# Consecutive dense products to different PSUM banks in a two-layer hybrid network on one core

## The chip, the cores and the metric

The kernel runs on one core of a Trainium2 chip. The metric is the device time of one execution in microseconds (us); the same program was run three times, and one more execution was recorded by the hardware profiler.

## What is computed

Two layers over 256 tokens of 1024 features, in float32. Each layer adds half of a gated feed-forward network, then a mixer, then half of another feed-forward network to `x`:

```python
def swiglu(h, w_gu, w_down):
    g, u = jnp.split(h @ w_gu, 2, axis=-1)
    return (jax.nn.silu(g) * u) @ w_down
...
for l in range(DEPTH):
    x = x + 0.5 * swiglu(rmsnorm(x, ffn1_norm[l]), ffn1_w_gu[l], ffn1_w_down[l])
    ...
    x = x + mix
    x = x + 0.5 * swiglu(rmsnorm(x, ffn2_norm[l]), ffn2_w_gu[l], ffn2_w_down[l])
```

`w_gu` is 1024 x 5632 and `w_down` 2816 x 1024. The even layer's mixer is a gated product along the tokens beside a differential attention; the odd layer's is a latent attention beside a grouped one. Each mixer has one input product from the normed `x` and one output product with a 1024 x 1024 matrix.

## The kernel before

**Accuracy.** TensorE multiplies operands of a float32r type with about 12 bits. So every weight and every activation is split into an upper part (`hi`, or part 0) and the rest (`lo`, or part 1), and a product a·w is summed from three: upper by upper, upper by lower, lower by upper.

**Products.** `dense(b, xh, xl, wh, wl, ...)` issues these three one after the other into one PSUM bank `b`. `wide(b, wh, wl, x2, ...)` does the same with two instructions: the weights' upper part against both parts of the activations side by side (512 columns, filling a bank), then the weights' lower part against the activations' upper part (256 columns, added to the bank's second half). A bank holds 512 float32 a partition; there are eight, named `bank_124` to `bank_131` in the orders below.

**Stages.** A feed-forward network has two. The *gate-up* stage (`ffn`, first loop) takes four tiles of 128 columns at a time, four banks: for each of 8 tiles k of the normed input `xs`, it calls `wide` for each of the four. The *down* stage (second loop) takes one tile t of 128 output features at a time, one bank, and calls `wide` for each of 22 tiles k of the gated values `hs`, which lie in the tile `region`. `evac` and `add` empty the banks on ScalarE and VectorE. `add` writes `x`, and then `after` (`normed`) makes the next stage's `xs` tile and adds to the sum of squares. A mixer's input product (`block`) has one bank for each half of the tokens; for each k it calls `dense` for the first half, then for the second. `out_product` has four banks, two output tiles to a bank, and goes through the rows of the weights in two halves p, all eight tiles t in each. `small` holds two further products of the odd mixer.

**Weights** stream from DRAM by 1 MB loads on SP's queue, in the order in which they are used; ScalarE (`hi`) and VectorE (`lo`) split them by pieces of 1024 elements a partition into two rings of six tiles. A piece has eight chunks of 128 x 128, and `chunk(ids, c)` finds a stream's c-th.

**Order.** All operations are recorded first; `Program.schedule` then starts them by priority and readiness, with a cost for each, and `emit` issues them from one line (L285 before), which is why all rows of the profile have that line. What stands in `prog.together()` stays together on its engine: one call of `dense` or `wide` before. Operations that empty banks, and those of the attentions, have a lead of 20 us over products in their priority.

Of the kernel before, what the change touches and what calls it, by code (L numbers as in the profile page):

```python
# [21 lines left out]
N = 256         # tokens  # L22
# [4 lines left out]
# rsqrt: the first guess's factor, and the constant that yields the guess  # L27
FACTOR, GUESS = 1.5 ** 0.2, 520464320.0

# the order of the mixers' parts: blocks of the input product, heads of the attentions  # L30
EVEN = "k q v u b d10 d00 d11 d01"
ODD = "q k g00 c u0 u1 g01 g11 m00 g10 m10 m01 m11"
SUB, PIECE = 2048, 1024         # elements a partition of a load of weights, and of a piece of it
RAW, RING = 4, 6                # tiles for loads, for pieces
T1, T2 = 6, 9                   # scratch tiles of 256 and of 512 elements
ARENA, ARENA32 = 11264, 5472    # elements a partition for what one part of the network keeps
MOST, SPARE = (6, 8), 2         # banks held by dense products and by others; those kept for the next in turn
# how far operations go before products (ns): those that empty banks, those of attention, the splits of weights
LEAD, LEAD_A, LEAD_W = 20e3, 20e3, 10e3
PATIENCE = 500.0                # for how long VectorE leaves a copy to ScalarE (ns)  # L40
WARM = 8

# columns of gcol: gains that run along the partitions
GC = {"norm": 0, "cq": 48, "bs": 51, "sub": 59, "mq": 60, "mk": 61}
NGC = 64
# columns of grow: gains that run along the free axis, on every partition
GR = {"evq": (0, 64), "evk": (64, 64), "mq": (128, 32), "mk": (160, 32), "gq": (192, 64), "gk": (256, 64), "lam": (320, 256)}
NGR = 576
# columns of rope: cos, -sin, sin of each kind of position
# [3 lines left out]
# ---- operations are recorded, then emitted in the order in which a list scheduler starts them  # L53
class Slot:
    """a view of a tile whose place the scheduler has still to choose among those of its kind"""
# [14 lines left out]
class Kind:  # L70
    """tiles of one size: how many, and how many of them are kept for the next in the recorded order"""
# [10 lines left out]
class Program:  # L82
    """Operations in an order that is right, with what each reads and writes; emitted by priority and readiness."""

    def __init__(self):
        self.ops = []
        self.writer, self.readers = {}, {}
        self.clock = 0.0   # the products' time so far: the base of the priorities
        self.spans = {}
        self.group = None  # L90
        self.slots = {}    # name -> [operations on it, kind, the first of them]
# [70 lines left out]
    def schedule(self):  # L162
        """-> the operations in the order of their starts, and the place of each slot"""
# [12 lines left out]
        wait = {e: [] for e in engs}     # by the time they are ready  # L176
        ready = {e: [] for e in engs}    # by priority
# [16 lines left out]
        def when(o, t):  # L194
            """the time from which the slots that o opens have places, or None"""
# [94 lines left out]
class Engine:  # L290
    """records the calls of one engine's instructions, each with the time that it takes (ns)"""
# [39 lines left out]
class Either:  # L331
    """copies that ScalarE or VectorE can make: the scheduler chooses"""
# [19 lines left out]
def trunk_kernel(ctx: ExitStack, tc: tile.TileContext, a: dict, out: bass.AP):  # L352
# [9 lines left out]
    def lead(ns):  # L362
        """the operations in here go before products recorded up to ns ahead of them"""
# [8 lines left out]
    # ---- memory: fixed tiles, some of them taken in turn  # L372
# [16 lines left out]
    class Arena:  # L389
        """what the parts of the network keep in one region, one part after the other"""  # L390
# [9 lines left out]
    class Taken:  # L400
        """scratch tiles of one kind"""
# [50 lines left out]
    with lead(90e3):  # L452
        # the tensor engine's clock rises with its use: it is kept busy while the first loads are under way
# [4 lines left out]
    # ---- the stream of weights: loaded, then split into two parts of 12 bits each  # L458
    loads, pieces, raws, ready = [], [], [], []

    def load(ap, widths):
        """-> the pieces' numbers"""
# [8 lines left out]
    def first(raw, w, n):  # L471
        """the first two loads of weights, in parts and among those of x"""
# [27 lines left out]
    def weight(i):  # L500
        fetch(i)
        return ready[i]

    # ---- pieces of arithmetic
    def rsqrt(y, s, scale, tile=None):
        """y = (s * scale + EPS) ** -0.5: a guess from the exponent, then a step of third order and one of Newton's.
        The guess is too large by the factor that makes the first step's leading coefficient 1."""
# [13 lines left out]
    def sums(ss, src, scale, n, w):  # L521
        """sums of squares of scale * src over each head's w, src [P, n * w]"""
# [4 lines left out]
    def rsqrt_of(srcs, scales, n, w):  # L527
        """[P, 2, n]: each head's 1 / rms of scale * src, for the two halves"""
# [5 lines left out]
    def split(dst_hi, dst_lo, src, gain=None):  # L534
        """the parts of src, times the gain of each partition"""
# [7 lines left out]
    def dense(b, xh, xl, wh, wl, first, last):  # L543
# [607 lines left out]
```

## Time and profile before

| | us |
|---|---|
| median of three runs | 947.79 (947.45 to 948.05) |
| profiled execution, span from its first to its last instruction | 946.8 |
| two feed-forward stages of it, gate-up and down, from the middle of the run | 122.3 and 62.2 |

The page gives for each engine its busy time and its share of the span; matmuls (PE) and the loads of their stationary operand (PEld) stand apart. A row of the timeline gives the start, the duration and the instruction, written as output<-inputs; a matmul's duration includes its passage through the array, so that neighbours overlap. The page has no time of the profiled execution other than its span.

### The profile page before, as it was taken

How to read it: one execution, taken by the hardware profiler on the slowest of the kernel's cores; microseconds unless marked ns; L12 is line 12 of the kernel's file. 1: busy time of each engine (PE TensorE's matmuls, PEld its weight loads, DVE VectorE, ACT ScalarE, POOL GpSimd, SP SyncE). 2: the span in 40 equal slices, each digit the busy share in tenths (PEclk: the TensorE clock that was granted, in tenths of full speed). 3: DMA queues.
4: the chain of work that ended last, by engine and by line, in shares of the span. 5: the costliest groups of instructions: out<-in, count | busy, mean ns of one | idle time of the engine just before them, and what ended most of it. 6: DMA issues, size and time to landing. Idle time of an engine off the chain costs nothing.

```text
span 946.8 us, 14519 instructions
## 1 busy us (share of the span) xinstructions
PE 938.2 (99%) x5564; PEld 825.4 (87%) x5564; DVE 729.8 (77%) x1332; ACT 546.0 (58%) x932; POOL 29.5 (3%) x57
## 2 busy tenths in 40 slices
PE   8999999999999999999999999999999999999998
PEld 7888888888899888888888888888989988888887
DVE  7997776679989878876688887766888698887651
ACT  7765654446956666654455656544487566565430
POOL 0920000000000000000000000000000000000000
PEclk9999999999999999999999999999999999999999
DMA  8775555553254555555555555554512355555530
GB/s 319 272 262 182 181 197 196 184 178 134 95 214 170 190 188 205 185 178 184 197 179 197 181 202 197 178 183 154 184 59 84 107 185 199 178 192 207 192 107 17
DMA packets 26421, 167.83 MB, mean 177 GB/s; under 512 B 2928, under 2 KB 5104, under 8 KB 7024
## 3 DMA queue, kind: packets, MB, share of 16 engines
q1 hardware_dynamic: 26352, 166.92, 50.1%
q8 instruction: 43, 0.70, 0.3%
q14 instruction: 26, 0.21, 0.1%
HBM read 165.86 MB, written 1.05 MB: 176 GB/s over the span
## 4 chain that ended last, share of the span: by engine, by line
PE 96%; DVE 1%; DMA 1%; ACT 1%; issue 0%; SPq 0%; DVEq 0%; ACTq 0%
PE bank L285 96%; DMA gx<-in_gx 1%; ACT t L285 1%; DVE t L285 0%; DVE sm L285 0%; DVE lo L285 0%; SPq L285 0%; DVE acc L285 0%; DVE region L285 0%; DVE hi L285 0%; ACT L285 0%; ACT hi L285 0%; ACT xs L285 0%; DVE ssg L285 0%; DVE gx L285 0%
## 5 line engine op out<-in xcount | busy, mean ns | idle before, releaser
L285 ACT ACTIVATE hi<-raw 128x1024 fp32r<-128x1024 f32 (+3 forms) x310 | 322.8, 1043 | 316.8 <-PE bank L285 199.0
L285 DVE TENSOR_TENSOR lo<-raw,hi 128x1024 fp32r<-128x1024 f32 (+2 forms) x318 | 382.5, 1204 | 155.9 <-ACT hi L285 150.3
L285 PE MATMUL bank<-xs,hi 128*128 128x512 f32 x1408 | 489.0, 392 | 1.1 <-ACT hi L285 1.1
L285 PE MATMUL bank<-xs,lo 128*128 128x256 f32 x1408 | 394.0, 280 | 1.6 <-DVE lo L285 1.6
L285 PEld LDWEIGHTS bank<-xs,hi 128*128 128x128 f32 x1408 | 264.4, 188 | 59.5 <-ACT hi L285 1.6
L285 PE MATMUL bank<-region,hi 128*128 128x512 f32 (+1 forms) x982 | 296.6, 364 | 0.0
L285 PEld LDWEIGHTS bank<-xs,lo 128*128 128x128 f32 x1408 | 264.3, 188 | 2.9 <-DVE lo L285 2.9
L285 PE MATMUL bank<-region,lo 128*128 128x256 f32 x832 | 234.0, 281 | 0.0
L285 PEld LDWEIGHTS bank<-region,hi 128*128 128x128 f32 x982 | 174.9, 189 | 32.1
L285 PEld LDWEIGHTS bank<-region,lo 128*128 128x128 f32 x832 | 157.6, 189 | 0.0
L285 ACT ACTIVATE t<-bank 128x256 f32<-128x256 f32 (+1 forms) x201 | 76.4, 399 | 38.9 <-PE bank L285 37.9
L285 PE MATMUL bank<-hi,xs 128*128 128x512 f32 (+2 forms) x256 | 78.6, 381 | 0.0
L285 DVE TENSOR_TENSOR t<-bank,t 128x256 f32<-128x256 f32 x176 | 67.2, 419 | 0.4 <-ACT t L285 0.4
L285 DVE TENSOR_TENSOR t<-t,rb 128x512 f32<-128x512 f32 x88 | 60.2, 688 | 1.2
L285 DVE SCALAR_TENSOR_TENSOR gx<-bank,gx 128x256 f32<-128x256 f32 (+1 forms) x71 | 32.1, 452 | 33.6 <-PE bank L285 32.8
L285 PEld LDWEIGHTS bank<-hi,xs 128*128 128x128 f32 x256 | 47.1, 188 | 8.6
L285 PE MATMUL bank<-lo,xs 128*128 128x512 f32 (+2 forms) x128 | 48.0, 375 | 0.0
L285 DVE TENSOR_TENSOR t<-t,t 128x256 f32<-128x256 f32 (+2 forms) x108 | 45.8, 428 | 0.1
L285 ACT ACTIVATE t<-t 128x256 f32<-128x256 f32 (+2 forms) x98 | 39.0, 406 | 3.2 <-DVE t L285 3.1
L285 DVE TENSOR_TENSOR region<-t,region 128x256 fp32r<-128x256 f32 (+2 forms) x92 | 39.1, 429 | 1.2 <-ACT region L285 1.2
L285 ACT ACTIVATE region<-t 128x256 fp32r<-128x256 f32 (+1 forms) x89 | 35.5, 404 | 1.6 <-DVE t L285 1.4
L285 PEld LDWEIGHTS bank<-lo,xs 128*128 128x128 f32 x128 | 24.1, 188 | 3.8
(130 smaller groups left out, 466.4 us busy)
## 6 DMA issues: line engine op xcount, KB each, us to landing
raw<-in_gu SPq DMA_DIRECT2D x86, 1024.0 KB, 4.8
raw<-in_dn SPq DMA_DIRECT2D x44, 1024.0 KB, 4.8
raw<-in_ev_in SPq DMA_DIRECT2D x10, 1024.0 KB, 4.9
raw<-in_ev_out SPq DMA_DIRECT2D x4, 1024.0 KB, 5.0
raw<-in_od_out SPq DMA_DIRECT2D x4, 1024.0 KB, 4.7
raw<-in_gu SPq DMA_DIRECT2D x8, 256.0 KB, 5.3
raw<-in_od_q SPq DMA_DIRECT2D x2, 1024.0 KB, 4.7
raw<-in_od_c SPq DMA_DIRECT2D x2, 832.0 KB, 4.4
```

The lines of the kernel that those rows point to most:

```text
L285: r = fn(*map(real, args), **{k: real(v) for k, v in kw.items()})
```

## The change

`dense` takes several sums at once and lets them take turns, product by product; `wide` takes several banks, and issues all upper products and then all lower ones, each of the two as a group that stays together. `block` and `small` hand both halves of the tokens to `dense`; the gate-up stage hands its four tiles to `wide`; the down stage takes two tiles at a time (the last two tiles of the last network stay single); `out_product` takes tiles in the order 0 2 1 3 4 6 5 7, two of different banks at a time, and empties two banks after the fourth tile and two after the eighth. The layouts `_down` and `_out` put the weights in the order of this use. All comments and docstrings are gone as well, which moves the issuing line to L286.

```diff
+OUT = [0, 2, 1, 3, 4, 6, 5, 7]
...
-    def dense(b, xh, xl, wh, wl, first, last):
+    def dense(*sums):
         with prog.together():
             c = 0.0
-            for l, r, s, e in ((xh, wh, first, False), (xh, wl, False, False), (xl, wh, False, last)):
-                c += T.matmul(b, lhsT=l, rhs=r, start=s, stop=e)
+            for z in range(3):
+                for b, xh, xl, wh, wl, first, last in sums:
+                    l, r = ((xh, wh), (xh, wl), (xl, wh))[z]
+                    c += T.matmul(b, lhsT=l, rhs=r, start=first and z == 0, stop=last and z == 2)
         prog.clock += c
...
-    def wide(b, wh, wl, x2, first, last):
+    def wide(banks, ws, x2, first, last):
+        c = 0.0
         with prog.together():
-            c = T.matmul(b, lhsT=wh, rhs=flat(x2), start=first, stop=False)
-            c += T.matmul(b[:, 1, :], lhsT=wl, rhs=x2[:, 0, :], start=False, stop=last)
+            for b, (wh, _) in zip(banks, ws):
+                c += T.matmul(b, lhsT=wh, rhs=flat(x2), start=first, stop=False)
+        with prog.together():
+            for b, (_, wl) in zip(banks, ws):
+                c += T.matmul(b[:, 1, :], lhsT=wl, rhs=x2[:, 0, :], start=False, stop=last)
...
-        for t in range(KT):
-            b = bank(2, N)
-            parts = 1 if after is finish and t == KT - 1 else 2
+        ends = KT - 2 if after is finish else KT
+        for ts in [(t, t + 1) for t in range(0, ends, 2)] + [(t,) for t in range(ends, KT)]:
+            banks = [bank(2, N) for _ in ts]
+            parts = 1 if ts == (KT - 1,) else 2
             for k in range(FT):
-                w = chunk(dn, FT * t + k)
+                ws = [chunk(dn, FT * ts[0] + len(ts) * k + z) for z in range(len(ts))]
...
-def _down(w):
-    return _chunks(w.reshape(FT, P, KT, P).transpose(2, 0, 1, 3))
+def _down(w, last):
+    t = w.reshape(FT, P, KT, P).transpose(2, 0, 1, 3)
+    ends = KT - 2 if last else KT
+    two = t[:ends].reshape(-1, 2, FT, P, P).swapaxes(1, 2).reshape(-1, P, P)
+    return _chunks(np.concatenate([two, t[ends:].reshape(-1, P, P)]))
```

TensorE's order at the first gate-up stage, before (a row is output<-operands and the moving operand's size; `hi_112` and `lo_118` are the two parts of one weight piece):

```order
L285 MATMUL bank_125<-xs,hi_112 128x512
L285 MATMUL bank_125<-xs,lo_118 128x256
L285 MATMUL bank_126<-xs,hi_112 128x512
L285 MATMUL bank_126<-xs,lo_118 128x256
L285 MATMUL bank_127<-xs,hi_112 128x512
L285 MATMUL bank_127<-xs,lo_118 128x256
L285 MATMUL bank_128<-xs,hi_112 128x512
L285 MATMUL bank_128<-xs,lo_118 128x256
```

and after:

```order
L286 MATMUL bank_125<-xs,hi_112 128x512
L286 MATMUL bank_126<-xs,hi_112 128x512
L286 MATMUL bank_127<-xs,hi_112 128x512
L286 MATMUL bank_128<-xs,hi_112 128x512
L286 MATMUL bank_125<-xs,lo_118 128x256
L286 MATMUL bank_126<-xs,lo_118 128x256
L286 MATMUL bank_127<-xs,lo_118 128x256
L286 MATMUL bank_128<-xs,lo_118 128x256
```

Each bank had its 512-column and its 256-column product in turn; now four of the one stand ahead of four of the other. In the down stage two of the one stand ahead of two of the other, in two banks, where all 44 products of a tile stood in one bank.

TensorE's order in an input block of the even mixer, before (`bank_129` and `bank_130` are the two halves of the tokens):

```order
L285 MATMUL bank_130<-hi_112,xs 128x512
L285 MATMUL bank_130<-lo_118,xs 128x512
L285 MATMUL bank_130<-hi_112,xs 128x512
L285 MATMUL bank_129<-hi_113,xs 128x512
L285 MATMUL bank_129<-lo_119,xs 128x512
L285 MATMUL bank_129<-hi_113,xs 128x512
```

and after (the halves are `bank_131` and `bank_129`):

```order
L286 MATMUL bank_131<-hi_113,xs 128x512
L286 MATMUL bank_129<-hi_113,xs 128x512
L286 MATMUL bank_131<-lo_119,xs 128x512
L286 MATMUL bank_129<-lo_119,xs 128x512
L286 MATMUL bank_131<-hi_113,xs 128x512
L286 MATMUL bank_129<-hi_113,xs 128x512
```

Three products in a row went to one bank; now the bank changes at each.

TensorE's order in the odd mixer where the latent attention's products (384 columns) meet the grouped attention's first heads, before (`region` 128x256 are scores, `ident` is a transpose, 128x65 are sums over values):

```order
L285 MATMUL bank_127<-region 128x256 x6
L285 MATMUL bank_128<-hi_114,region 128x384
L285 MATMUL bank_128<-lo_120,region 128x384
L285 MATMUL bank_128<-hi_114,region 128x384
L285 MATMUL bank_131<-region 128x256 x6
L285 MATMUL bank_128<-hi_114,region 128x384
L285 MATMUL bank_128<-lo_120,region 128x384
L285 MATMUL bank_128<-hi_114,region 128x384
L285 MATMUL bank_125<-ident,t_7_74 128x128 x4
L285 MATMUL bank_124<-hi_114,region 128x384
L285 MATMUL bank_124<-lo_120,region 128x384
```

and after:

```order
L286 MATMUL bank_127<-lo_120,region 128x384
L286 MATMUL bank_125<-lo_120,region 128x384
L286 MATMUL bank_127<-hi_114,region 128x384
L286 MATMUL bank_125<-hi_114,region 128x384
L286 MATMUL bank_130<-ident,t_7_74 128x128 x4
L286 MATMUL bank_126<-ident,t_1_68 128x128 x4
L286 MATMUL bank_130<-region_133,t_8_75 128x65 x4
L286 MATMUL bank_130<-region_133,t_7_74 128x65 x4
L286 MATMUL bank_126<-ident,t_5_72 96x128 x4
L286 MATMUL bank_127<-ident,t_6_73 128x128 x4
L286 MATMUL bank_125<-ident,t_2_69 96x128 x4
```

Groups of three dense products stood between pieces of the attention; now all twelve are done before the attention's transposes, which then follow without dense products between them.

More of the change, by code (lines that the diff above doesn't have):

```diff
@@ L617, in block @@
         for k in range(KT):
-            for h in range(2):
-                hi, lo = weight(ids[k // per])
-                c = slice(k % per * w, k % per * w + w)
-                dense(banks[h][:, :w], xs[:, k, 0, half(h)], xs[:, k, 1, half(h)], hi[:, c], lo[:, c], k == 0, k == KT - 1)
+            hi, lo = weight(ids[k // per])
+            c = slice(k % per * w, k % per * w + w)
+            dense(*((banks[h][:, :w], xs[:, k, 0, half(h)], xs[:, k, 1, half(h)], hi[:, c], lo[:, c], k == 0, k == KT - 1)
+                    for h in range(2)))
         with lead(LEAD):
@@ L643, in out_product @@
         for p in range(2):
-            for t in range(KT):
+            for n in range(4):
+                ts = OUT[2 * n:2 * n + 2]
                 for k in range(4):
-                    wh, wl = chunk(ids, 32 * p + 4 * t + k)
                     i = 4 * p + k
-                    dense(banks[t // 2][:, t % 2, :], wh, wl, os_[:, 0, i, :, :], os_[:, 1, i, :, :],
-                          i == 0 and t % 2 == 0, i == KT - 1 and t % 2 == 1)
-                if p == 1 and t % 2 == 1:
-                    add(flat(banks[t // 2]), t - 1, 2, 1.0, after)
+                    dense(*((banks[t // 2][:, t % 2, :], *chunk(ids, 32 * p + 8 * n + 2 * k + z), os_[:, 0, i, :, :],
+                             os_[:, 1, i, :, :], i == 0 and t % 2 == 0, i == KT - 1 and t % 2 == 1) for z, t in enumerate(ts)))
+                if p == 1 and n % 2 == 1:
+                    for t in ts:
+                        add(flat(banks[t // 2]), t - 1, 2, 1.0, after)
     def finish(k):
@@ L674, in ffn @@
             for k in range(KT):
-                for t in range(4):
-                    wide(banks[t], *chunk(gu, 16 * j + 4 * k + t), xs[:, k], k == 0, k == KT - 1)
+                wide(banks, [chunk(gu, 16 * j + 4 * k + t) for t in range(4)], xs[:, k], k == 0, k == KT - 1)
             with lead(LEAD):
@@ L679, in ffn @@
                     evac(j + t, *banks[2 * t:2 * t + 2])
-        for t in range(KT):
-            b = bank(2, N)
-            parts = 1 if after is finish and t == KT - 1 else 2
+        ends = KT - 2 if after is finish else KT
+        for ts in [(t, t + 1) for t in range(0, ends, 2)] + [(t,) for t in range(ends, KT)]:
+            banks = [bank(2, N) for _ in ts]
+            parts = 1 if ts == (KT - 1,) else 2
             for k in range(FT):
-                w = chunk(dn, FT * t + k)
+                ws = [chunk(dn, FT * ts[0] + len(ts) * k + z) for z in range(len(ts))]
                 if parts == 1:
-                    dense(b[:, 0, :], *w, hs[:, k, 0], hs[:, k, 1], k == 0, k == FT - 1)
+                    dense((banks[0][:, 0, :], *ws[0], hs[:, k, 0], hs[:, k, 1], k == 0, k == FT - 1))
                 else:
-                    wide(b, *w, hs[:, k], k == 0, k == FT - 1)
-            for z in reversed(range(parts)):
-                add(b[:, z, :], t, 1, 0.5, after if z == 0 else None)
+                    wide(banks, ws, hs[:, k], k == 0, k == FT - 1)
+            for t, b in zip(ts, banks):
+                for z in reversed(range(parts)):
+                    add(b[:, z, :], t, 1, 0.5, after if z == 0 else None)
     def rotate(dst, src, tt, h, heads, w):
@@ L954, in small @@
             for k in range(2):
-                for h in range(2):
-                    c = slice(384 * k, 384 * k + 384)
-                    dense(qs[h][:, :384], cT[h][:, 0, k, :], cT[h][:, 1, k, :], hi[:, c], lo[:, c], k == 0, k == 1)
+                c = slice(384 * k, 384 * k + 384)
+                dense(*((qs[h][:, :384], cT[h][:, 0, k, :], cT[h][:, 1, k, :], hi[:, c], lo[:, c], k == 0, k == 1)
+                        for h in range(2)))
             hi, lo = weight(w[f"u{n}"][1])
-            for h in range(2):
-                dense(ks[h], cT[h][:, 0, 2, :], cT[h][:, 1, 2, :], hi[:, :512], lo[:, :512], True, True)
+            dense(*((ks[h], cT[h][:, 0, 2, :], cT[h][:, 1, 2, :], hi[:, :512], lo[:, :512], True, True) for h in range(2)))
             with lead(LEAD):
@@ L1072, in _gate_up @@
     return _chunks(w.reshape(KT, P, 2, FT // 2, 2, P).transpose(3, 0, 4, 2, 1, 5))
-def _down(w):
-    return _chunks(w.reshape(FT, P, KT, P).transpose(2, 0, 1, 3))
+def _down(w, last):
[3 more added lines that the diff above has]
+    return _chunks(np.concatenate([two, t[ends:].reshape(-1, P, P)]))
 def _out(w):
-    return _chunks(w.reshape(2, 4, P, KT, P).transpose(0, 3, 1, 2, 4))
+    t = w.reshape(2, 4, P, KT, P).transpose(0, 3, 1, 2, 4)[:, OUT]
+    return _chunks(t.reshape(2, 4, 2, 4, P, P).swapaxes(2, 3))
 def _rope():
@@ L1121, in layouts @@
     r["gu"] = np.stack([_gate_up(i[f"ffn{f}_w_gu"][l]) for l in range(2) for f in (1, 2)])
-    r["dn"] = np.stack([_down(i[f"ffn{f}_w_down"][l]) for l in range(2) for f in (1, 2)])
+    r["dn"] = np.stack([_down(i[f"ffn{f}_w_down"][l], (l, f) == (1, 2)) for l in range(2) for f in (1, 2)])
     r["ev_in"] = _blocks(i["ev_w_in"][0], 512, 4)
```

## The prediction

> **What bounds the kernel now.** I read the page's first two parts, then the chain that ended last, then TensorE's waits.
>
> ```profile
> PE 938.2 (99%) x5564; PEld 825.4 (87%) x5564; DVE 729.8 (77%) x1332; ACT 546.0 (58%) x932; POOL 29.5 (3%) x57
> PEclk9999999999999999999999999999999999999999
> ...
> PE 96%; DVE 1%; DMA 1%; ACT 1%; issue 0%; SPq 0%; DVEq 0%; ACTq 0%
> ```
>
> ```profile
> PE bank L285 <- DVE lo L285: 1.6, 3, 1.1
> PE bank L285 <- ACT hi L285: 1.1, 2, 0.7
> PE bank L285 <- DVE ones L446: 1.1, 1, 1.1
> PE bank L285 <- ACT t L285: 0.3, 1, 0.3
> PE bank L285 <- DVE region L285: 0.2, 1, 0.2
> ```
>
> TensorE is busy 99% of the span, holds 96% of the chain, and waits 4.3 us in all (1.6 + 1.1 + 1.1 + 0.3 + 0.2). So the kernel is one stream of matmuls, and the question is whether the change makes that stream denser. The granted clock is full in all slices, so the clock hides nothing. "Busy" itself tells little, because matmuls overlap: what counts is the time from one start to the next. I take it from the timeline (start, duration, instruction), as the first and the last row of long stretches.
>
> ```profile
> 289.15 0.39 PE L285 MATMUL bank<-xs,hi 128*128 128x512 f32 x1
> ...
> 411.43 0.39 PE L285 MATMUL bank<-region,hi 128*128 128x512 f32 x1
> ...
> 473.60 0.39 PE L285 MATMUL bank<-xs,hi 128*128 128x512 f32 x1
> ```
>
> From 289.15 to 411.43 lies one gate-up stage: 352 pairs of a 512-column product (with `hi`) and a 256-column product (with `lo`), and two products for the rms. The stage takes 122.28 us; the two extra ones at about 0.12 us leave 122.04, or 346.7 ns a pair. From 411.43 to 473.60 lies one down stage, 176 pairs of the same two widths: 62.17 us, 353.2 ns a pair.
>
> ```profile
> 411.60:473.50 61.90, 61.90 (x352) 53.68 (x352) 41.38 (x60) 29.04 (x40) 0.00 (x0) 1.00 0.52 186
> ...
> 690.00:722.00 32.00, 31.25 (x219) 27.37 (x217) 29.27 (x101) 26.51 (x56) 0.00 (x0) 1.00 0.20 67
> ```
>
> In the windows (length, then the busy time of PE, PEld, DVE and ACT) the down stage has no gap on TensorE; the odd mixer's middle has 0.75 us of gaps in 32.00.
>
> **The main term: bank changes between neighbours.** In the built order of before, 3439 steps from one dense product to the next stay in their bank and 1570 change it; after the change 108 stay and 4906 change. So whatever a same-bank step costs is taken away 3331 times. What does it cost? The gate-up stage changes bank at every second step, the down stage at 9 steps of 351, and the pair is 346.7 against 353.2 ns. Taken alone, that says that a same-bank step costs 6.5 ns. Three other stretches let me test this.
>
> ```profile
> 277.51 0.28 PE L285 MATMUL bank<-region,lo 128*128 128x256 f32 x1
> ...
> 289.03 0.28 PE L285 MATMUL bank<-region,lo 128*128 128x256 f32 x1
> ```
>
> ```profile
> 198.30 0.40 PE L285 MATMUL bank<-lo,xs 128*128 128x512 f32 x1
> ...
> 215.34 0.39 PE L285 MATMUL bank<-hi,xs 128*128 128x512 f32 x1
> ```
>
> The first two rows bound 96 products of 256 columns in the output product, which nearly all stay in their bank: 11.52 us, 120.0 ns each. The other two bound 73 products of 512 columns in an input block, where, as the order shows, **every third step changes bank**: 17.04 us, 233.4 ns each. Now 120.0 + 233.4 = 353.4, which is the down stage's pair without bank changes. Had each change in the block saved 6.5 ns, its mean would be 2.2 ns lower, and the stretch 0.16 us shorter; the rows resolve 0.02 us. Inside the down stages, too, the rhythm of starts runs through the steps from one tile's bank to the next. So single bank changes save nothing that this trace shows, and the gate-up stage must be faster for another reason. It differs from the rest in its moving operand: `xs` begins 32 bytes past a multiple of 64 in the built program, while `region` and the weight pieces begin on multiples, and the change leaves these places alone. I can't prove that this is the reason, but it fits all four stretches. I take **0** for this term; the bounds are −22 us (rival A) and +9 us (rival B).
>
> The Trainium skill, page "TensorE: Matmul & The Clock Gate", section "Back-to-back issue gap", gives N / 2.4 + 2.5 ns between two isolated warm matmuls, which would be 215.8 + 109.2 = 325 ns for such a pair. By it the two kinds of stage would lose 1408 × 21.7 + 682 × 28.2 ns = 50 us, an estimate. No stretch of this trace runs at that pace, the bank changes in the block do not come nearer to it, and the page ties the difference to no bank; its chance is 0. The page "Perfetto Trace Analysis", section "Matmuls" under "Optimizing Tensor Performance", wants independent groups to rotate through banks so that the evacuation of one overlaps the next. By that rule the change would earn what TensorE waits for evacuation; the waits above name no such wait, so the sum by it is 0 as well.
>
> **The regrouping.** Instruction counts, widths, bytes and loads stay; only order and layout of the weights change.
>
> Start: the first gate-up groups wait for split weights.
>
> ```profile
> 18.36 0.40 PE L285 MATMUL bank<-xs,hi 128*128 128x512 f32 x1
> 19.87 0.39 PE L285 MATMUL bank<-xs,lo 128*128 128x256 f32 x1 [1.12 <-DVE lo L285]
> ```
>
> Four `hi` products now stand ahead of the first `lo`, where one stood. When `lo` is late, three more products of 0.23 us (0.69 us) run in the meantime. The waits for `lo` are 1.6 us in all, so the gain lies between 0 and 1.6; since the arrival of the weights sets the last of these waits, I take that wait alone, **−0.7 us**.
>
> Ends of stages: two tiles of a down stage now end together, and four of the output product.
>
> ```profile
> L285 DVE SCALAR_TENSOR_TENSOR gx<-bank,gx 128x256 f32<-128x256 f32 x63 | 26.6, 423 | 32.3 <-PE bank L285 31.4
> L285 DVE SCALAR_TENSOR_TENSOR gx<-bank,gx 128x512 f32<-128x512 f32 x8 | 5.5, 687 | 1.3 <-PE bank L285 1.3
> L285 DVE SCALAR_TENSOR_TENSOR xs<-gx,xs 128x256 fp32r<-128x256 f32 x48 | 22.9, 480 | 2.5 <-ACT xs L285 2.3
> L285 DVE TENSOR_TENSOR acc<-acc,t 128x256 f32<-128x256 f32 x42 | 17.6, 420 | 0.2
> L285 DVE TENSOR_TENSOR lo<-raw,hi 128x1024 fp32r<-128x1024 f32 x302 | 369.6, 1225 | 149.5 <-ACT hi L285 144.2
> ```
>
> After the last output product VectorE has 2 × 0.69 + 4 × (0.48 + 0.42) = 5.0 us of work, and at most one split of 1.2 us ahead of it. The cover is the next gate-up: it reads `xs` tile k after 4k pairs, so tile 4 at 16 × 0.347 = 5.5 us and tile 7 at 9.7 us. Tile 4 is ready after about 2.5 us. The down stage's end has 4 × 0.42 + 2 × 0.90 = 3.5 us for tiles that are read from 8.3 us on. Without that cover the two output products would each expose about 5 us. **0.**
>
> Mixers: a dense group among the attentions is now six products and not three. In the odd mixer the order has 16 stretches of dense products where it had 22, and its longest stretches without any grow from 46 to 70 instructions. TensorE executes in order, so a transpose that waits for an exponential holds back whatever follows.
>
> ```profile
> 687.78 2.64 PE L285 MATMUL bank<-region 64*128 64x256 f32 x35 [0.16 <-DVE region L285]
> ...
> 696.84 1.11 PE L285 MATMUL bank<-region,t 128*128 128x65 f32 x8 [0.30 <-ACT t L285]
> ```
>
> Today such waits are 0.16 and 0.30 us. Six lost fillers at 0.16 to 0.30 us give 1.0 to 1.8 us if each one exposes such a wait, and nothing if the other heads fill in. Below nothing the most is the 0.5 us of waits there now. I take **+0.7 us**, between nothing and the nearest rows. The bank pressure that comes with it (two banks held in the down stage and not one) has no row; with no wait for a bank in before I take 0, and count its upper side into rival C.
>
> Sum against the profiled span: 946.8 + 0 − 0.7 + 0 + 0.7 = 946.8 us. The median of the runs, 947.79, is 1.0 us above the span, so 947.8; as the start's gain is the surer of the two small terms I say **947.5 us**.
>
> **The rivals.**
>
> A, banks pay after all once every step changes: 3331 steps × 6.5 to 6.7 ns (120.0 and 353.3 against 346.7) = 22 us, 925.5 us. For it: gate-up against down. Against it: the 73 products above. Chance 0.20. A smaller form, in which only a `hi` after a `lo` in the same bank costs (644 such steps before, 21 after): 623 × 6.6 ns = 4 us, 943.5 us, 0.08.
>
> B, slower: equal widths in a row cost the gate-up stage its advantage. Its place is the four `hi` and four `lo` that now follow each other; its price is the pair at the block's 233.4 plus the output product's 120.0 instead of 346.7, so 6.7 ns × 1408 pairs = 9.4 us, 957 us. It decides as soon as the first undisturbed gate-up stage reads 124.6 us and not 122.3. For it: the only runs of equal width in this trace have these paces. Against it: the down stage alternates widths and has the same pace, so alternation isn't what makes gate-up fast. 0.10.
>
> C, slower: the coarser groups starve the odd mixer.
>
> ```profile
> L285 DVE TENSOR_REDUCE sm<-bank 128x2 f32<-128x512 f32 x24 | 16.1, 681 | 1.0 <-PE bank L285 1.0
> ```
>
> ```profile
> L285 ACT ACTIVATE t<-bank,sm,scm 128x256 f32<-128x256 f32 x16 | 8.0, 573 | 2.5 <-DVE sm L285 2.5
> ```
>
> Half a softmax is one reduction and two exponentials, 0.68 + 2 × 0.57 = 1.8 us. Where it comes to lie open in both of the longest attention stretches, that is 3.6 us, with some switching 4 us: 951.5 us. For it: the stretches of 65 and 70 instructions; against it: about 120 dense products still stand behind the last attention there, so the heads are not last. 0.12.
>
> D, the waits shrink further than I take, at the start and among the heads: all 1.6 and 0.5 us, 945.5 us, 0.04.
>
> That the change doesn't do what it says is excluded by the counts: 108 same-bank steps of 5014 are left.
>
> **How the numbers follow.** The forecast, no change, has 0.46, its own range 945.9 to 949.5. A difference within 0.2% (1.9 us) can hardly be told from none here. Faster: 0.20 + 0.08 + 0.04 = 0.32. Slower: 0.10 + 0.12 = 0.22. The range goes from A, with a little below it, to C: 924 to 952. It leaves out B and the far ends.
>
> **What would show it.** The first undisturbed gate-up stage (352 pairs) at 122.3 us and a down stage at 62.2 us say that the main term is 0. A down stage of 60 us and gate-up of 120 say A; 124.6 for gate-up says B. TensorE's waits name the start (`DVE lo` below 1.6 us) and the mixers (`ACT t`, `DVE region` above 0.5 us says C). The forecast fails if bank changes that save nothing one by one save something in a row, or if the order of widths matters to the pace.

## The result and the profile after

| | before | changed |
|---|---|---|
| median, five runs each, us | 947.88 (947.45 to 948.31) | 954.67 (954.28 to 959.29) |
| ratio, with its 95% interval | 1 | 1.0081 (1.0062 to 1.0099) |
| profiled execution, us | span 946.8 | 959.29, span 957.5 |

The change makes the kernel 0.8% slower. The page of the changed kernel has the same instruction count on TensorE and a longer span. Its first part, the clock's row of the second part and the chain's row of the fourth:

```profile
PE 946.2 (99%) x5564; PEld 831.1 (87%) x5564; DVE 742.9 (78%) x1405; ACT 534.3 (56%) x859; POOL 28.3 (3%) x57
PEclk9999999999999999999999999999989999999999
PE 95%; DVE 2%; DMA 1%; ACT 0%; SPq 0%; issue 0%; ACTq 0%; DVEq 0%
```

TensorE still is the bound. It is 8 us longer busy with the same 5564 matmuls, and one slice of the clock's row, at three quarters of the span, is no longer full. What it waits for (in all, times, longest, us):

```profile
PE bank L286 <- DVE region L286: 2.1, 2, 1.4
PE bank L286 <- ACT t L286: 1.8, 3, 1.2
PE bank L286 <- ACT hi L286: 1.3, 2, 0.9
PE bank L286 <- DVE ones L447: 1.1, 1, 1.1
PE bank L286 <- DVE t L286: 0.8, 1, 0.8
PE bank L286 <- ACT region L286: 0.3, 1, 0.3
```

The waits have grown from 4.3 to 7.4 us. `DVE lo` is gone from the list; `DVE region` and `ACT t`, which belong to the attentions, have gone from 0.5 to 3.9 us. The stage boundaries in the timeline of the changed kernel (start, duration, instruction):

```profile
289.82 0.63 PE L286 MATMUL bank<-xs,hi 128*128 128x512 f32 x2
...
414.10 0.63 PE L286 MATMUL bank<-region,hi 128*128 128x512 f32 x2
...
475.42 0.63 PE L286 MATMUL bank<-xs,hi 128*128 128x512 f32 x2
...
661.04 0.63 PE L286 MATMUL bank<-hi,xs 128*128 128x512 f32 x2
...
767.71 0.39 PE L286 MATMUL bank<-xs,hi 128*128 128x512 f32 x1
```

The gate-up stage from 289.82 takes 124.28 us where it took 122.28, the down stage after it 61.32 where it took 62.17, and the odd mixer from 661.04 to 767.71 takes 106.67 where it took 100.22. Worked out in the same way for the whole program, from first start to first start, in us:

| | first gate-up | each later gate-up (3) | each down (3) | even mixer | odd mixer | last down | tail |
|---|---|---|---|---|---|---|---|
| before | 126.07 | 122.28 | 62.17 | 95.73 | 100.22 | 54.40 | 7.80 |
| changed | 128.77 | 124.29 | 61.32 | 94.45 | 106.67 | 53.62 | 7.79 |

(The last down stage is counted as its first seven tiles; the tail is the eighth, up to the start of its last product.) The differences, 2.7 + 3 x 2.0 - 3 x 0.85 - 1.3 + 6.4 - 0.8, add up to 10.5 of the 10.7 us between the two spans. So no part of the program stands still: two kinds of stage pay, two cost.

In the odd mixer of the changed kernel TensorE waits (in brackets, with the releaser):

```profile
689.12 1.35 PE L286 MATMUL bank<-ident,t 128*128 128x128 f32 x8 [0.28 <-ACT t L286]
690.76 0.38 PE L286 MATMUL bank<-region 64*128 64x256 f32 x1 [0.30 <-ACT region L286]
691.80 2.63 PE L286 MATMUL bank<-region 64*128 64x256 f32 x35 [0.66 <-DVE region L286]
...
699.37 3.47 PE L286 MATMUL bank<-region,t 128*128 128x65 f32 x16 [1.24 <-ACT t L286]
...
729.38 0.70 PE L286 MATMUL bank<-region 96*128 96x256 f32 x2 [1.41 <-DVE region L286]
```

and the windows around that place (length, busy time of PE, PEld, DVE, ACT and POOL, granted clock, DMA share, GB/s) show what follows:

```profile
690.00:699.50 9.50, 7.00 (x62) 5.84 (x61) 9.09 (x40) 7.83 (x24) 0.00 (x0) 1.00 0.00 1
699.60:706.40 6.80, 6.80 (x34) 6.70 (x34) 5.31 (x14) 4.25 (x10) 0.00 (x0) 0.50 0.41 154
706.50:767.60 61.10, 59.62 (x459) 56.26 (x459) 40.49 (x112) 39.42 (x75) 0.00 (x0) 1.00 0.24 80
```

In 9.50 us TensorE was idle for 2.50. Then, for 6.8 us, the granted clock was 0.50, which costs half of that, 3.4 us. The rest of the stage's 6.4 us is waits: in the first two windows and the third, 2.5 + 1.5 us of gaps, against 0.7 + 0.2 in the same part of the stage before.

The timed runs lose less here than the profiled one: their mean granted clock is 0.998 and not 0.994, and 0.004 x 957 = 3.8 us is most of the 4.6 us by which the profiled span is longer than their middle one, 952.9.

### The profile page after: what moved, and what is told of

Same layout as the page of the kernel before. It is cut to its first block, busy times and chain, and to the rows that moved or that the text cites. A ratio compares the mean times of both kernels' runs of the same rounds, so it can differ in the third digit from the quotient of the medians.

```text
span 957.5 us, 14504 instructions
## 1 busy us (share of the span) xinstructions
PE 946.2 (99%) x5564; PEld 831.1 (87%) x5564; DVE 742.9 (78%) x1405; ACT 534.3 (56%) x859; POOL 28.3 (3%) x57
## 3 DMA queue, kind: packets, MB, share of 16 engines
HBM read 165.86 MB, written 1.05 MB: 174 GB/s over the span
## 4 chain that ended last, share of the span: by engine, by line
PE 95%; DVE 2%; DMA 1%; ACT 0%; SPq 0%; issue 0%; ACTq 0%; DVEq 0%
PE bank L286 95%; DMA raw<-in_gu 1%; DVE sm L286 1%; DVE t L286 0%; DVE lo L286 0%; ACT t L286 0%; SPq L286 0%; DVE region L286 0%; DVE acc L286 0%; DVE hi L286 0%; ACT hi L286 0%; DVE gx L286 0%; ACT region L286 0%; DVE rc L286 0%; DVE ssc L286 0%
## 5 line engine op out<-in xcount | busy, mean ns | idle before, releaser
L286 ACT ACTIVATE hi<-raw 128x1024 fp32r<-128x1024 f32 (+2 forms) x313 | 326.2, 1043 | 327.2 <-PE bank L286 264.5
L286 DVE TENSOR_TENSOR lo<-raw,hi 128x1024 fp32r<-128x1024 f32 (+2 forms) x318 | 381.1, 1200 | 134.0 <-ACT hi L286 133.3
L286 PE MATMUL bank<-xs,hi 128*128 128x512 f32 x1408 | 387.4, 397 | 1.3 <-ACT hi L286 1.3
L286 PEld LDWEIGHTS bank<-xs,hi 128*128 128x128 f32 x1408 | 240.7, 188 | 33.8 <-ACT hi L286 1.8
L286 PE MATMUL bank<-region,hi 128*128 128x512 f32 (+1 forms) x982 | 265.2, 362 | 0.0
L286 PEld LDWEIGHTS bank<-xs,lo 128*128 128x128 f32 x1408 | 217.6, 190 | 31.9
L286 PE MATMUL bank<-xs,lo 128*128 128x256 f32 x1408 | 224.9, 282 | 0.0
L286 PEld LDWEIGHTS bank<-region,lo 128*128 128x128 f32 x832 | 152.2, 188 | 29.3
L286 PE MATMUL bank<-region,lo 128*128 128x256 f32 x832 | 167.8, 279 | 0.0
L286 PEld LDWEIGHTS bank<-region,hi 128*128 128x128 f32 x982 | 146.8, 189 | 1.2
L286 PE MATMUL bank<-hi,xs 128*128 128x512 f32 (+2 forms) x256 | 68.9, 380 | 0.0
L286 DVE TENSOR_TENSOR t<-bank,t 128x256 f32<-128x256 f32 x176 | 66.4, 416 | 2.5 <-ACT t L286 1.3
L286 DVE TENSOR_TENSOR t<-t,rb 128x512 f32<-128x512 f32 x88 | 57.0, 685 | 0.0
L286 DVE COPY t<-bank 128x256 f32<-128x256 f32 (+1 forms) x81 | 34.4, 426 | 28.5 <-PE bank L286 28.4
L286 ACT ACTIVATE t<-t 128x256 f32<-128x256 f32 (+2 forms) x98 | 40.1, 415 | 28.1 <-DVE t L286 28.1
L286 PEld LDWEIGHTS bank<-hi,xs 128*128 128x128 f32 x256 | 45.5, 188 | 8.0
L286 ACT ACTIVATE t<-bank 128x256 f32<-128x256 f32 (+1 forms) x123 | 43.9, 406 | 9.2 <-PE bank L286 8.9
L286 DVE TENSOR_TENSOR t<-t,t 128x256 f32<-128x256 f32 (+2 forms) x108 | 45.8, 427 | 0.5 <-ACT t L286 0.3
L286 ACT ACTIVATE region<-t 128x256 fp32r<-128x256 f32 (+1 forms) x88 | 36.8, 420 | 15.6 <-DVE t L286 15.3
L286 DVE SCALAR_TENSOR_TENSOR gx<-bank,gx 128x256 f32<-128x256 f32 (+1 forms) x71 | 27.6, 446 | 17.8 <-PE bank L286 17.7
L286 DVE TENSOR_TENSOR region<-t,region 128x256 fp32r<-128x256 f32 (+2 forms) x92 | 38.8, 426 | 0.1
L286 PE MATMUL bank<-lo,xs 128*128 128x512 f32 (+2 forms) x128 | 37.8, 376 | 0.0
```

Of the source, the lines that this page charges most:

```text
L286: r = fn(*map(real, args), **{k: real(v) for k, v in kw.items()})
```

## The experiments

Three explanations were open for the gate-up and down stages: banks, the order of widths, and the place of the moving operand. The odd mixer had the waits and the clock.

**Patterns of dense products by themselves (m1_patterns).** No network: 26 stretches of 96 products on weights of the first gate-up.

```diff
+    # 11 every step changes bank A
+    for d, l, r, s, e in seq(wA, mA, 1, 4, 4, banks, step=1):
+        K(nc.tensor.matmul(d, lhsT=l, rhs=r, start=s, stop=e))
...
```

The operand `mA` begins on a multiple of 64 bytes, `mB` 32 bytes past one.

> Leaves the network out: 26 stretches of 96 products each on random data, every stretch from a line of its own; output is x. Operand places: A begins on a multiple of 64 bytes, B 32 bytes past one; 'n:n' is n products of 512 columns, then n of 256. Theory 1 (place of the moving operand): every stretch on A has 353.3 ns a pair (120.0 for 256, 233.3 for 512 alone), every one on B less, near 346.7, whatever the banks and the order. Theory 2 (order of widths): the pace follows the order and not the place: 346.7 for 1:1, about 348.3 for 2:2, about 352.5 for 4:4, 353.3 from equal widths alone, the same on A and B and for one bank or four. Theory 3 (banks): stretches in one bank are slower than the same stretch in four, on A as on B: 353.3 against 346.7 for 1:1, 560 cycles and fewer for 512 columns alone.

The groups view gives, for each stretch, its count, the busy time and the mean ns of one. As the products follow each other without a gap, the busy time of a group of 512-column products is the stretch's length but for the last 256-column product:

```profile
L151 PE MATMUL bank<-mB,wh 128*128 128x512 f32 x96 | 22.6, 395 | 0.0
L154 PE MATMUL bank<-mB,wh 128*128 128x512 f32 x96 | 22.6, 395 | 0.0
L145 PE MATMUL bank<-mA,wh 128*128 128x512 f32 x96 | 22.0, 390 | 0.0
L148 PE MATMUL bank<-mA,wh 128*128 128x512 f32 x96 | 21.9, 389 | 0.0
...
L184 PE MATMUL bank<-mA,wh 128*128 128x512 f32 x48 | 17.0, 399 | 0.0
L181 PE MATMUL bank<-mA,wh 128*128 128x512 f32 x48 | 17.0, 399 | 0.0
...
L130 PE MATMUL bank<-mB,wh 128*128 128x512 f32 x48 | 16.7, 390 | 0.0
L187 PE MATMUL bank<-mB,wh 128*128 128x512 f32 x48 | 16.7, 390 | 0.0
```

L145 and L151 put all 96 products in one bank, L148 and L154 go round four: no difference beyond 0.1 us. L181 and L130 are pairs in one bank, L184 and L187 change bank at every step: none either. What moves the pace is the place (17.0 against 16.7 us for 48 pairs, the other way round, 22.0 against 22.6, for 96 products of 512 columns alone) and, by the starts in the timeline, the order of widths. In ns for one 512-column and one 256-column product, from the ninth start of a stretch to the 89th:

| | pairs | two by two | four by four |
|---|---|---|---|
| moving operand on a multiple of 64 bytes | 353.5 | 348.3 | 350.8 |
| 32 bytes past one | 346.7 | 346.7 | 349.8 |

One place disagrees with this table: pairs on a multiple of 64 in one bank with a new operand at each pair ran at 346.6. With the weights shifted by 32 bytes as well, the places change roles (pairs 346.7 with an unshifted operand, 353.3 with a shifted one), so what counts is where the operand lies relative to the weights. The order isn't a matter of banks either: two by two on a multiple of 64 ran at 348.3 in one bank and in two, four by four 32 bytes past one at 350.0 in one bank and 349.8 in four. Banks cost nothing; place and order both count.

**Gate-up back to pairs (e1_gateup_pairs).** The changed kernel, but the gate-up stage issues `hi` and `lo` of one bank together as before.

```diff
+        if len(banks) == 4:
+            for z in range(4):
+                wide(banks[z:z + 1], ws[z:z + 1], x2, first, last)
+            return
...
```

> The changed kernel with the gate-up stage back to one bank's pair after the other; the down stage, the mixers and the layouts as changed. If the order of widths in gate-up lost the 2.0 us a stage: undisturbed gate-up stages at 122.3 us, down stages at 61.3 us, time about 8 us under the changed kernel's 954.7, so 946.5. If banks or something else made gate-up slower: 124.3 us a stage and 954.7. What the mixers lose stays in either case.

947.70 us, 1.2 above what was expected, ratio to before 0.9996 (0.9985 to 1.0006). Timeline of this kernel, the same gate-up stage:

```profile
288.33 0.39 PE L286 MATMUL bank<-xs,hi 128*128 128x512 f32 x1
...
410.61 0.62 PE L286 MATMUL bank<-region,hi 128*128 128x512 f32 x2
```

The stage is back at 122.28 us, though half of its steps stay in their bank again. So the four-by-four order alone makes the gate-up stage slower (m1 excludes that the bank changes do it). The odd mixer still takes 103.75 us, again with a stretch at half the clock:

```profile
686.60:690.00 3.40, 3.40 (x34) 3.40 (x33) 3.25 (x15) 1.61 (x2) 0.00 (x0) 0.50 0.01 2
```

It stands behind shorter waits than in the changed kernel, by the timeline of this one:

```profile
683.56 1.34 PE L286 MATMUL bank<-ident,t 128*128 128x128 f32 x8 [0.28 <-ACT t L286]
685.20 0.38 PE L286 MATMUL bank<-region 64*128 64x256 f32 x1 [0.29 <-ACT region L286]
686.24 4.14 PE L286 MATMUL bank<-region 64*128 64x256 f32 x35 [0.66 <-DVE region L286]
```

Three waits of 1.23 us in all came before it; 0.5 us of waits in the kernel before brought none.

**Dense sums one by one in the mixers (e3_mixers_single).** The changed kernel, but each sum of `dense` stays a group of three of its own.

```diff
+        sums = list(sums)
+        if len(sums) > 1:
+            for s in sums:
+                dense(s)
+            return
```

> The changed kernel with every dense sum a group of its own again (input blocks, output products, the odd mixer's small products), in one bank at a time as before; gate-up and down as changed. If the coarser groups starve the odd mixer and its clock: the odd mixer back from 106.7 to about 100.3 us in the profile, no slice of the granted clock under 9 there, time about 952 (the timed runs had less of the dip than the profiled one). If the loss there comes from elsewhere, the odd mixer stays over 104. If bank changes helped blocks and output products, these would get slower by up to 0.16 us in 73 products; if not, 233.3 and 120.0 ns stay.

952.50 us, ratio 1.0041 (1.0028 to 1.0054). The odd mixer takes 100.28 us, as before the change, between these rows of the timeline:

```profile
659.63 0.40 PE L286 MATMUL bank<-hi,xs 128*128 128x512 f32 x1
...
759.91 0.63 PE L286 MATMUL bank<-xs,hi 128*128 128x512 f32 x2
```

The window where the waits were (same columns as above):

```profile
690.00:710.00 20.00, 19.41 (x155) 16.86 (x154) 17.76 (x60) 18.17 (x42) 0.00 (x0) 1.00 0.15 53
```

and from the timeline of the same kernel:

```profile
698.40 1.11 PE L286 MATMUL bank<-region,t 128*128 128x65 f32 x8 [0.29 <-ACT t L286]
```

No stretch of half clock is left, and this is the longest wait there. The gate-up stage stays at 124.30 us and the down stage at 61.31; the even mixer returns to 95.76, so its gain of 1.3 us came from the turns in `dense`, too. It isn't a gain of the dense products: by their starts, the 240 of the blocks take 57.3 us before and 57.2 in the changed kernel and the 192 of the output product 23.4 in both, though the bank now changes at each step; the 148 products of the gating and the attention between them take 13.8 us instead of 15.1.

**The place alone (e4_xs_aligned).** The kernel before, with `xs` 32 bytes further on, on a multiple of 64.

```diff
-    xs = keep("xs", KT, 2, N, dt=F32R)
+    xs = sb.tile([P, 8 + KT * 2 * N], F32R, name="xs")[:, 8:].rearrange("p (k z n) -> p k z n", k=KT, z=2)
```

> The kernel before, with xs begun 32 bytes further on, so on a multiple of 64. If the place of the moving operand makes gate-up fast: 353.3 ns a pair, 124.6 us a stage, time about 957. If it doesn't: 122.3 us a stage and 947.9.

956.52 us, ratio 1.0086 (1.0070 to 1.0101). The gate-up stage in the timeline of this kernel:

```profile
289.75 0.40 PE L285 MATMUL bank<-xs,hi 128*128 128x512 f32 x1
...
414.36 0.39 PE L285 MATMUL bank<-region,hi 128*128 128x512 f32 x1
```

124.61 us: 353.3 ns a pair, the down stage's pace, in the order of before, but for the two products for the rms, which come two pairs earlier. The gate-up stage owed its speed to where `xs` happened to lie.

**How far the place reaches (m2_places).** No network; pairs in one bank, with the moving operand at several offsets, other reuse, and fewer columns of weights.

```diff
+    # 1:1, 32 bytes
+    for d, l, r, s, e in seq(w, mv(0, 8), 1, 1, 4, banks):
...
+    # 1:1, 0 bytes, 4 pairs, a quarter of the weights' columns
+    for d, l, r, s, e in seq(w, mv(0, 0), 1, 1, 4, banks, cols=32):
...
```

> Leaves the network out: 26 stretches of 96 products in one bank each, on random data, a source line to each stretch; the weights' parts begin on multiples of 64 bytes, the moving operand 0 to 128 bytes further. If the place relative to the weights within 64 bytes sets the pace (what the first patterns and the aligned xs showed): 353.3 ns a pair of 1:1 at 0, 64 and 128 bytes and 346.7 at 32, with the other places between them or like 32; 512 columns alone 226.7 ns at 0 and 233.3 at 32, 256 columns alone 120.0 at 0 and 117.8 at 32. If the cause is that the load of the next weights reads at the same time as the moving operand: with half and a quarter of the weights' columns the excess over 325 ns a pair shrinks, to a half and a quarter if it goes by columns. If it is a matter of the moving operand alone, the weights' columns change nothing. A moving operand that is new for every pair at 0 bytes ran at 347 in the first patterns though the kernel's down stage ran at 353.3: with 22 in turn it either follows the kernel (353.3) or the pattern (347).

In ns a pair, by the same starts: 351.2 at offset 0, 353.3 at 8, 346.9 at 16, 355.6 at 24, **346.7 at 32**, 355.0 at 40, 350.0 at 48, 351.1 at 56, 353.4 at 64 and 353.2 at 128 bytes. A new operand at each pair or at each fourth made no difference here (351.2). One width alone missed what was expected: 512 columns ran at 232.3 ns at offset 0 and 234.2 at 32 (226.7 and 233.3 in m1), 256 columns at 118.6 and 118.7 (120.0 and 117.8). Groups with all, half and a quarter of the weights' columns:

```profile
L110 PE MATMUL bank<-mv,wh 128*128 128x512 f32 x48 | 16.9, 393 | 0.0
...
L185 PE MATMUL bank<-mv,wh 128*32 128x512 f32 x48 | 16.8, 395 | 0.0
...
L122 PE MATMUL bank<-mv,wh 128*128 128x512 f32 x48 | 16.7, 392 | 0.0
L173 PE MATMUL bank<-mv,wh 128*64 128x512 f32 x48 | 16.7, 392 | 0.0
L176 PE MATMUL bank<-mv,wh 128*64 128x512 f32 x48 | 16.7, 392 | 0.0
L179 PE MATMUL bank<-mv,wh 128*32 128x512 f32 x48 | 16.4, 388 | 0.0
```

At offset 0 (L110, L173, L179) fewer columns shorten the pair from 351.2 to 346.7 and 340.0 ns; at 32 bytes (L122, L176, L185) they don't: 346.7, 346.6, 349.1. So the number of weight columns counts at one place and hardly at the other. With it go both the load of the weights and the rows of the output, and that two reads get in each other's way is a guess that this run does not settle.

**Region moved as well (b1_region_moved, b3_both).** The kernel before, and the version b2 below, with `region` 32 bytes on, so that the down stage has the good place, too.

```diff
-    region, region32 = keep("region", ARENA, dt=F32R), keep("region32", ARENA32)
+    region, region32 = keep("region", ARENA + 16, dt=F32R)[:, 8:8 + ARENA], keep("region32", ARENA32)
```

> The kernel before, with region (the down stage's and output products' moving operand) begun 32 bytes further on, xs where it was. If place sets the pace: down stages at 346.7 ns a pair, 61.0 us instead of 62.2, output products at 117.8 ns instead of 120.0, all in all 4.4 + 0.8 us less: 942.7. If only xs matters: 947.9.

> The same with region begun 32 bytes further on. If place sets the pace also of paired tiles (2:2 ran at 347.9 with the operand 32 bytes off and at 349.6 without in the first patterns): down stages at 61.0 us and output products at 117.8 ns, so about 2 us under the kernel with the paying parts, 941. If paired tiles have had all that is to be had: the same as that kernel.

Both missed: 962.92 us, ratio 1.0162 (1.0148 to 1.0176), and 961.93, ratio 1.0152 (1.0138 to 1.0166). The down stage in b1's timeline, between the last two of these rows, did what was expected:

```profile
293.24 0.40 PE L285 MATMUL bank<-xs,hi 128*128 128x512 f32 x1
...
417.83 0.40 PE L285 MATMUL bank<-region,hi 128*128 128x512 f32 x1
...
478.85 0.39 PE L285 MATMUL bank<-xs,hi 128*128 128x512 f32 x1
```

It took 61.02 us. But the edit did two other things. The tile is 64 bytes longer, so `xs`, which lies behind it, moved from 32 to 96 bytes past a multiple of 128, and the gate-up stage, with its products in the order of before, took 124.60 us: 32 and 96 bytes are not the same place, so it counts modulo 128 bytes at least. And the kernel records what an operation touches in blocks of 16 elements, which the shift by 8 elements cuts, so that operations which meet in a cut block count as dependent. From the even mixer on, TensorE's order is another than before: the mixers took 99.6 and 107.4 us, with three stretches of 3.4 us at half the clock. (The 347.9 and 349.6 ns in b3's expectation stand as 346.7 and 348.3 in the table of m1.)

**The parts that paid (b2_parts_that_paid).** The changed kernel with gate-up in pairs and single sums in the odd mixer only; left are the two-by-two down stage and the even mixer's turns.

```diff
+        sums = list(sums)
+        if len(sums) > 1 and single[0]:
+            for s in sums:
+                dense(s)
+            return
...
     def odd(w, w_out, after):
+        single[0] = True
...
```

> The changed kernel with gate-up by pairs and the odd mixer's dense sums single, so of the change only the paired down tiles and the even mixer's turns are left. If the parts add up: gate-up 122.3, down 61.3, even mixer 94.4, odd mixer 100.3, no half-speed slice of the clock, so 947.9 - 3 x 0.85 - 0.8 - 1.3 = 943.2. If the clock's dips belong to something else in the change: over 945.

943.03 us, ratio 0.9953 (0.9940 to 0.9965). Its code differs from e1's in the odd mixer alone: 0.9996 - 0.9953 = 0.0043 (give or take 0.0016 by the two intervals), or 4.1 us, is what the coarser groups cost in timed runs, with what the start happened to differ by. One timed run of e1 had the full clock, and its span was 944.1 us against the 941.0 of b2's profile; so some 3 us of the 4.1 are waits and the rest is the clock.

**The place, moved cleanly (c1_paid_and_place, c2_place_alone).** b2, and the kernel before, with `region` moved by a tile of padding ahead of it and a second one behind it, so that `xs` keeps its place modulo 128 bytes and no block is cut.

```diff
-    region, region32 = keep("region", ARENA, dt=F32R), keep("region32", ARENA32)
+    keep("pad0", 8)
+    region = keep("region", ARENA, dt=F32R)
+    keep("pad1", 24)
+    region32 = keep("region32", ARENA32)
```

> The kernel of the parts that paid, with region moved 32 bytes by a small tile ahead of it and xs moved by 128 bytes in all, so that both begin 32 bytes past a multiple of 128 and the order of operations stays. If the place within 128 bytes sets the pace: gate-up stages stay at 122.3 us, down stages go from 61.3 to 61.0, the 384 products of 256 columns in the mixers' output products from 120.0 to about 117, so 943.0 - 1.1 - 1.2 = 940.7. If the loss of the first move of region came from something other than xs's place and the dependencies: gate-up at 124.6 again and over 955.

> The kernel before, its order untouched, with the same two places. If place alone gives the down stage what two tiles in turn gave it: down stages at 61.0 us instead of 62.2, gate-up at 122.3, output products at about 117 ns, 947.7 - 4.5 - 1.2 = 942.0. If the down stage needs other banks or another order: 947.7.

c1: 940.67 us, ratio 0.9921 (0.9910 to 0.9933), the fastest of all. c2: 941.90 us, ratio 0.9934 (0.9922 to 0.9946), with every instruction in the order of before. Timeline of c1:

```profile
285.58 0.40 PE L286 MATMUL bank<-xs,hi 128*128 128x512 f32 x1
...
407.86 0.63 PE L286 MATMUL bank<-region,hi 128*128 128x512 f32 x2
...
468.89 0.39 PE L286 MATMUL bank<-xs,hi 128*128 128x512 f32 x1
```

Gate-up 122.28, down 61.03 us; c2 has 122.27 and 61.01. With the operand in the good place, two-by-two and pairs cost the same in the down stage, as in m1's table. Two padding tiles are worth a little more than all of the order's gains together (0.9934 against b2's 0.9953; the intervals overlap, the times, at most 942.2 and at least 942.8 us, do not).

**The changed kernel once more (a2_changed_again).** The same kernel, a second profile, to see what of the odd mixer comes back.

> The changed kernel once more, for a second profile. If the half-speed stretch of the clock in the odd mixer belongs to its waits: waits of 2 to 3 us there again and at least one such stretch behind them, the odd mixer between 103 and 107 us. If it was chance: no such stretch and about 102.5. Gate-up 124.3, down 61.3 and even mixer 94.4 us in either case.

957.06 us in its one execution, too few for a ratio. Gate-up 124.29, down 61.32, odd mixer 106.69; its windows:

```profile
697.70:704.60 6.90, 6.90 (x36) 6.80 (x35) 5.28 (x12) 4.74 (x11) 0.00 (x0) 0.51 0.43 154
690.00:697.70 7.70, 6.16 (x59) 5.43 (x57) 7.32 (x35) 6.15 (x12) 0.00 (x0) 1.00 0.00 0
```

The waits came again, 1.54 us of gaps in the 7.70 us ahead, and so did the 6.8 us at half the clock. The shorter stretch at the start of the program (3.4 us) that the first profile had is missing here.

## Why the prediction was wrong

**What held.** Bank changes save nothing: m1's one-bank and four-bank stretches agree, and the mixers' dense products kept their pace (e3). Rival A is out, in its smaller form, too. But the sum that spoke against it fitted by chance. The 233.4 ns came from products that move the weights past `xs`, the 120.0 from products that move `region`: two places, not one. With `xs` on a multiple of 64 (e4), the even mixer's longest stretch of block products, 75, runs at 230.2 ns instead of 234.5, and in m1 the two widths alone add up to 346.7 ns at the place where the pairs take 353.5, and to 351.1 where they take 346.7. The suspicion about the place of `xs` was right in e4 and c2, more exactly as a place relative to the weights and modulo 128 bytes or more (m2's 351.2 at 0 and 353.2 at 128 are for more). The ends of stages cost nothing, as worked out: the down and gate-up stages follow each other without a wait.

**The step that failed: the main term of 0.** It put "the change leaves these places alone" for "so the pace stays", and against rival B it argued that alternation could not be what makes gate-up fast, because the down stage alternates at the slower pace. That compared two stages that differ in place as well as in order, and so couldn't speak on order. The runs show that both count: at the place of `xs`, four by four costs 124.29 - 122.28 = 2.0 us a stage or 5.7 ns a pair (rival B took 6.7, from rows of one width alone), which is **6.0 us** over three stages. So rival B's mechanism came true, and its sign, 124.6 us a stage, nearly (124.3). At the place of `region`, two by two gains 0.85 us a stage, **-3.3 us** with the last one's 0.8; none of the cases had this. The prediction gave B 0.10 and C, which follows, 0.12, each by itself; that both came, and a gain against them, was in none of its cases, and its range left B out. The first gate-up stage tells less: with `xs` in its old place and no stretch at half clock it took 125.0 to 126.1 us in pairs (before, b2, c1, c2) and 126.2 and 126.6 four by four (e3, a2).

**Mixers, +0.7.** One gain and one size were missed. The even mixer gained 1.3 us, among the products between its dense ones (e3). In the odd one the mechanism was rival C's, a transpose or a product that holds back the stream while a softmax is still at work. C gave it 4 us; b2 against e1 gives 4.1 in timed runs, and the two profiles of the changed kernel 6.45 and 6.47. The waits are not all of it: "the clock hides nothing" was read from a profile with 0.5 us of such waits, and did not say what the clock does when they grow.

**Start, -0.7.** Not to be told from none. In its first 25 us, without the first wait of 1.05, TensorE waits 1.2 to 2.1 us in the three profiles with four by four (changed, a2, e3) and 1.3 to 2.8 in those with pairs (b2, c2, e4, c1, before, e1). The waits for `DVE lo` went away, but the group for the rms now stands ahead of the four `lo` and waits 0.8 us for VectorE's `t`, the last but one of the waits listed above. In the first profile of the changed kernel and in e1's, 3.4 us at half the clock follow there, at 1.7 us; in the second profile they don't.

**The sum.** 947.9 + 6.0 - 3.3 - 1.3 + 4.1 = 953.4 us from the experiments' terms, against 954.7 measured; 1.3 us remain, of the size by which the first gate-up stage differs and the stretches at half clock come and go.

**What stays open.** Why place and order of widths set the pace: the run with fewer columns speaks for the weights' loads at one offset and against them at the other, and the same pattern ran at 346.6 and 351.2 ns in m1 and m2, where the operand and the weights lie differently far apart. Of the 5.7 ns that four by four costs in the gate-up stage, the pattern by itself shows 3.1 (349.8 against 346.7). And how much waiting brings on half the clock is known only within bounds, as the last section says.

## What to carry to other kernels

When two stages with the same instructions run at different paces, list all that differs between them, addresses of the operands included, before one difference is cleared or blamed; a stretch of a hundred products by themselves separates them in one run, though its sizes need not be the kernel's (four by four cost 3.1 ns a pair there and 5.7 here). On this kernel, moving an operand tile by 32 bytes was worth some 6 us (ratio 0.9934) without touching the order, while coarser groups of dense work among dependent steps were paid for twice, in waits and then in clock.

## What the runs showed of the hardware

Pairs of a 512-column and a 256-column float32r product ran at 346.6 to 355.6 ns with 128 columns of weights, in one bank or several, depending on the offset of the moving operand in steps as small as 8 bytes and on the order of the widths (m1, m2).

The stretches at half the clock lasted 3.413 us, or twice that, 6.827, in every profile that had one before its last product. The Trainium skill, page "TensorE: Matmul & The Clock Gate", section "What's actually happening", gives the same 3413 ns for the window of the clock gate and has the clock fall after at least one idle window. On the second point the traces differ: ahead of the stretch in the changed kernel TensorE was idle for 2.50 us of 9.50, the longest single wait being 1.24 us, and in e1 for 1.23 us in three waits of at most 0.66; the single wait of 1.41 us at 729.38 in the changed kernel was followed by none. That is nearer to the same page's section "A second HAM failure mode: psum-queue depth-cycling", where frequent short idle times do it; here a few waits of one mixer did, and not a repeated cycle.

Within a profile these stretches begin whole multiples of 3.4133 us apart: 199 of them in the changed kernel (from 20.37 to 699.62), 195 in e1 (from 20.99 to 686.59), 125 and 15 in b1 (269.68, 696.34 and 747.54). So each trace can be cut into windows of that length. In the eleven profiles of the network, up to the last product, such a stretch begins after every window in which TensorE was idle for 1.54 us or more (six of them) and after none with 1.12 us or less. In between lie four windows with a stretch behind them (1.25 to 1.27 us) and windows of 1.24, 1.30 and 1.41 us without one. It therefore counts how the waits fall on the windows. The waits of 0.28, 0.29 and 0.66 us stand in one window in e1 (1.27 us with shorter gaps), and a stretch follows; in the changed kernel an edge lies behind the first of them, 0.99 us are left in the next window, and none follows. In the same way the waits at the start put 1.66 us into one window in the first profile of the changed kernel and 0.86 us in the second. Why a stretch lasts two windows in the changed kernel is open.
